# Dealing 1024 images to 128 partitions in two contiguous parts, with five loads, three stores and one more wait

## The chip, the cores and the metric

One core of a Trainium2 chip runs the kernel. The metric is device time in microseconds, the median of several executions. The kernel before takes 71.6 us. A change counts as faster or slower from 2% on.

A few words used throughout: a *transfer* is one load or store between HBM, the chip's main memory, and on-chip memory (SBUF); it is carried by 16 *transfer engines*, in *packets* (the 7 transfers of the kernel before make 1008 packets: for each, 128 of one partition's row and 16 of 4 bytes). Put in line by where one ends and the next begins, the 1008 records form 16 chains of 63, one for each engine: for each transfer 8 packets of a row and then one of 4 bytes (0.009 us), the transfers in the order of issue. The text calls this line of packets a *ring*; as the 16 are alike, it speaks of one. A transfer *lands* with the last of its 16 signals in the profile: those of the first load, whose last packets end at 8.88 to 9.25 us, come at 9.27 to 9.61 us. VectorE (DVE in the profile) is the engine that computes, SP the queue that issues the transfers. The *pitch* of a load is the distance in HBM between the rows of neighbouring partitions.

## The reference

```python
batch, channels, h, w = 16, 64, 32, 32
x        # (16, 64, 32, 32) float32
indices  # (16, 64, 32, 32), values 0 to 3; they reach the kernel as 64-bit integers
for b, c, i, j:                       # four nested loops
    idx = indices[b, c, i, j]
    output[b, c, 2 * i + idx // 2, 2 * j + idx % 2] = x[b, c, i, j]
# output: (16, 64, 64, 64) float32, zero elsewhere
```

There are 1024 images. One has 4 KiB of x, 8 KiB of indices and 16 KiB of result: 12 MiB to load in all and 16 MiB to store.

## The kernel before

Each partition has 8 images that lie together in HBM. For each of the four places in a 2x2 square, one VectorE instruction compares the indices with the place and multiplies by x. The parts that matter:

```python
G = 2; NG = T // G; FIRST = 3; N = H * W          # T = 8 images per partition
x_v = x.rearrange("b (ch t) h w -> (b ch) (t h w)", t=T)
idx_v = indices.rearrange("b (ch t) h w -> (b ch) (t h w)", t=T).bitcast(I32)
out_v = out.rearrange("b (ch g t) oh ow -> g (b ch) (t oh ow)", g=NG, t=G)
# ... (buffers and semaphores)
cut = FIRST * 2 * N
# issued ahead of the kernel's opening synchronisation, in this order:
nc.sync.dma_start(out=idx_t[:, :cut], in_=idx_v[:, :cut])     # 3 MiB, rows of 24 KiB, pitch 64 KiB
nc.sync.dma_start(out=x_t, in_=x_v)                           # 4 MiB, rows of 32 KiB
nc.sync.dma_start(out=idx_t[:, cut:], in_=idx_v[:, cut:])     # 5 MiB, rows of 40 KiB
# ... (semaphore increments and waits)
for t in range(T):                                 # one image, or two together
    for pidx in range(4):
        nc.vector.scalar_tensor_tensor(
            out=o_c[:, k : k + n, :, pidx // 2, :, pidx % 2],
            in0=idx_c[:, t : t + n], scalar=pidx, in1=x_c[:, t : t + n],
            op0=mybir.AluOpType.is_equal, op1=mybir.AluOpType.mult)
# ...
for g in range(NG):                                # four stores of two images per partition
    nc.sync.wait_ge(made, g + 1)
    nc.sync.dma_start(out=out_v[g], in_=out_t[g])
```

Of the kernel before, what the change touches and what calls it, by code (L numbers as in the profile page):

```python
# [1 line left out]

# [4 lines left out]

P = 128
F32 = mybir.dt.float32
I32 = mybir.dt.int32  # L10


class Program:




    def __init__(self, nc):
        self.nc = nc
        self.block = nc.main_func.blocks[0]  # L20
        self.kernel_block = nc.cur_bb.bb.name

    def __enter__(self):
        ins = self.block.instructions
        self.branches = [i for i in ins if "Branch" in type(i).__name__]
        n = len(ins) - len(self.branches)
        assert all("Branch" in type(ins[k]).__name__ for k in range(n, len(ins)))
        del ins[n:]
        self.nc.switch_bb(self.block.name, parent=None)
        self.symbolic = self.nc._always_lower_symbolic_ap  # L30
        self.nc._always_lower_symbolic_ap = False
        return self

    def first(self, made):
        ins = self.block.instructions
        assert ins[len(ins) - 1].name == made.ins.name
        moved = ins.pop()
        at = next(
            k
            for k, i in enumerate(ins)  # L40
            if i.engine == moved.engine and isinstance(i, mybir.InstDrain)
        )
        ins.insert(at, moved)

    def last(self, made):


        def move(nc):
            ins = self.block.instructions
            at = next(k for k, i in enumerate(ins) if i.name == made.ins.name)  # L50
            nc.main_func.blocks[-1].instructions.append(ins.pop(at))

        self.nc.at_finalize(move)

    def __exit__(self, kind, *_):
        self.nc._always_lower_symbolic_ap = self.symbolic
        if kind is None:
            for b in self.branches:
                self.block.instructions.append(b)
            self.nc.switch_bb(self.kernel_block, parent=None)  # L60


@with_exitstack
def kernel(
    ctx: ExitStack,
    tc: tile.TileContext,
    x: bass.AP,
    indices: bass.AP,
    kernel_size: bass.AP,
    out: bass.AP,  # L70
):
    nc = tc.nc
    assert kernel_size == 2

    B, C, H, W = x.shape
    n_img = B * C
    T = n_img // P
    assert T * P == n_img and C % T == 0

    G = 2  # L80
    NG = T // G
    FIRST = 3
    N = H * W
    x_v = x.rearrange("b (ch t) h w -> (b ch) (t h w)", t=T)
    idx_v = indices.rearrange("b (ch t) h w -> (b ch) (t h w)", t=T).bitcast(I32)
    out_v = out.rearrange("b (ch g t) oh ow -> g (b ch) (t oh ow)", g=NG, t=G)

    x_t = nc.alloc_sbuf_tensor("x_t", [P, T * N], F32).ap()
    idx_t = nc.alloc_sbuf_tensor("idx_t", [P, T * 2 * N], I32).ap()
    out_t = [  # L90
        nc.alloc_sbuf_tensor(f"out_t{g}", [P, G * 4 * N], F32).ap()
        for g in range(NG - 1)
    ]
    out_t.append(out_t[0])

    x_in = nc.alloc_semaphore("x_in")
    idx_in = [nc.alloc_semaphore(f"idx_in{g}") for g in range(2)]
    made = nc.alloc_semaphore("made")
    stored_0 = nc.alloc_semaphore("stored_0")
    stored = nc.alloc_semaphore("stored")  # L100

    x_c = x_t.rearrange("p (t i j) -> p t i j", t=T, j=W)
    idx_c = idx_t.rearrange("p (t i j two) -> p t i j two", t=T, j=W, two=2)[
        :, :, :, :, 0
    ]
    cut = FIRST * 2 * N

    with Program(nc) as program:
        program.first(
            nc.sync.dma_start(out=idx_t[:, :cut], in_=idx_v[:, :cut]).then_inc(  # L110
                idx_in[0], 16
            )
        )
        program.first(nc.sync.dma_start(out=x_t, in_=x_v).then_inc(x_in, 16))
        program.first(
            nc.sync.dma_start(out=idx_t[:, cut:], in_=idx_v[:, cut:]).then_inc(
                idx_in[1], 16
            )
        )

        nc.vector.wait_ge(x_in, 16).then_inc(x_in, -16)
        for t in range(T):
            g, k = t // G, t % G
            if t in (0, FIRST):
                half = int(t == FIRST)
                nc.vector.wait_ge(idx_in[half], 16).then_inc(idx_in[half], -16)  # L126


            if k == 1 and t != FIRST and g:
                continue  # L130
            n = 1 if k == 1 or t + 1 == FIRST or not g else 2
            if g == NG - 1:
                nc.vector.wait_ge(stored_0, 16).then_inc(stored_0, -16)
            o_c = out_t[g].rearrange(
                "p (m i two j wo) -> p m i two j wo", m=G, two=2, wo=2, j=W
            )
            for pidx in range(4):
                op = nc.vector.scalar_tensor_tensor(  # L138
                    out=o_c[:, k : k + n, :, pidx // 2, :, pidx % 2],
                    in0=idx_c[:, t : t + n],  # L140
                    scalar=pidx,
                    in1=x_c[:, t : t + n],
                    op0=mybir.AluOpType.is_equal,
                    op1=mybir.AluOpType.mult,
                )
            if k + n == G:
                op.then_inc(made, 1)

        for g in range(NG):
            nc.sync.wait_ge(made, g + 1)  # L150
            nc.sync.dma_start(out=out_v[g], in_=out_t[g]).then_inc(
                stored if g else stored_0, 16
            )
        nc.sync.sem_inc(made, -NG)
        program.last(
            nc.sync.wait_ge(stored, 16 * (NG - 1)).then_inc(stored, -16 * (NG - 1))
        )


# [1 line left out]
_INS = ['x', 'indices', 'kernel_size']  # L161
_OUTS = [((16, 64, 64, 64), 'float32')]

_NUMBERS = {'kernel_size': 2}


# [26 lines left out]
```

## Time and profile before

| | kernel before |
|---|---|
| device time, median | 71.6 us |
| span of the profiled execution | 70.2 us |
| share of the transfer engines' time that is filled | 97.6% |
| VectorE busy | 35.9 us |
| loads, stores | 3, 4 |

The prediction below shows the lines of the profile and reads them. In short: the ring of transfers is filled from 1 us to the end, from 5 us on at some 430 GB/s, and everything else is hidden behind it.

### The profile page before, as it was taken

What the parts mean: (1) busy time and instruction counts of PE and PEld (TensorE: products, weight loads), DVE (VectorE), ACT (ScalarE), POOL (GpSimd) and SP (SyncE); (2) the same over time, 40 slices, a digit from 0 to 9 for tenths busy, and PEclk for the clock granted to TensorE, in tenths of its full rate; (3) what the DMA queues carried; (4) which work ended last, traced back from release to release, by engine and by line L of the source; (5) the groups of instructions that cost most, each with busy time, mean ns of one, the idle gap of its engine ahead of it and who ended that gap; (6) DMA issues with size and microseconds to landing.
All of it is one profiled execution on the core that took longest, in us unless ns stands there. A gap on an engine that the chain in (4) does not pass through costs nothing.

```text
span 70.2 us, 76 instructions
## 1 busy us (share of the span) xinstructions
DVE 35.9 (51%) x24; POOL 0.2 (0%) x4
## 2 busy tenths in 40 slices
DVE  0000000000089999999999999999999500000000
POOL 1000000000000000000000000000000000000000
DMA  7699996979988899869999796969799896969692
GB/s 210 294 406 434 448 598 299 560 336 467 504 373 373 373 584 537 373 299 504 392 411 486 317 579 299 598 299 579 317 467 429 373 523 299 598 299 598 299 486 112
DMA packets 1008, 29.36 MB, mean 418 GB/s; under 512 B 112, under 2 KB 112, under 8 KB 112
## 3 DMA queue, kind: packets, MB, share of 16 engines
q1 hardware_dynamic: 1008, 29.36, 97.6%
HBM read 12.58 MB, written 16.78 MB: 418 GB/s over the span
## 4 chain that ended last, share of the span: by engine, by line
DVE 46%; DVEq 4%; issue 1%
DVE out_t L138 46%; DVEq L188 4%
## 5 line engine op out<-in xcount | busy, mean ns | idle before, releaser
L138 DVE SCALAR_TENSOR_TENSOR out_t<-idx_t,x_t 128x1024 f32<-128x1024 int32 (+1 forms) x24 | 35.9, 1574 | 19.6 <-DVEq L126 19.6
L174 POOL MEMSET const-bfloat16-1.0<- 128x1 bf16 x1 | 0.1, 101 | 0.0
L174 POOL MEMSET const-uint8-127<- 128x1 uint8 x1 | 0.1, 101 | 0.0
L174 POOL MEMSET const-float32-0.0<- 128x1 f32 x1 | 0.1, 98 | 0.2 <-issue 0.2
L174 POOL MEMSET const-float32-1.0<- 128x1 f32 x1 | 0.1, 98 | 0.0
## 6 DMA issues: line engine op xcount, KB each, us to landing
out_dram<-out_t SPq DMA_DIRECT2D x4, 4096.0 KB, 13.4
idx_t<-in_indices_dram SPq DMA_DIRECT2D x1, 5120.0 KB, 30.5
x_t<-in_x_dram SPq DMA_DIRECT2D x1, 4096.0 KB, 18.9
idx_t<-in_indices_dram SPq DMA_DIRECT2D x1, 3072.0 KB, 9.6
```

Source lines behind the costliest of these rows:

```text
L138: op = nc.vector.scalar_tensor_tensor(out=o_c[:, k : k + n, :, pidx // 2, :, pidx % 2], in0=idx_c[:, t : t + n], scalar=pidx, in1=x_c[:, t ...
L174: nc = _bacc.Bacc("TRN2", target_bir_lowering=False, num_devices=1)
L188: with _tile.TileContext(nc) as tc:
```

## The change

The intent, as the code has it, is to start VectorE earlier (after 4.5 MiB instead of 7), to make each part one contiguous piece of HBM with fewer and longer store packets, and to hold the first store back until the second-last load has landed.

```diff
-    x_v = x.rearrange("b (ch t) h w -> (b ch) (t h w)", t=T)
-    idx_v = indices.rearrange("b (ch t) h w -> (b ch) (t h w)", t=T).bitcast(I32)
-    out_v = out.rearrange("b (ch g t) oh ow -> g (b ch) (t oh ow)", g=NG, t=G)
+    A, Z = 3, 5
+    Z1, Z2 = 2, 3
+    def sections(ap):
+        flat = ap.rearrange("b ch h w -> (b ch) (h w)")
+        return [
+            part.rearrange("(p t) n -> p (t n)", t=t)
+            for part, t in ((flat[: A * P], A), (flat[A * P :], Z))
+        ]
     ... (one input buffer, in which the last results take the place of inputs)
+        for tile_, hbm, sem in (
+            (idx_a, idx_v[0], in_a),
+            (x_a, x_v[0], in_a),
+            (x_z, x_v[1], in_z),
+            (idx_z[:, :last_idx], idx_v[1][:, :last_idx], in_z),
+            (idx_z[:, last_idx:], idx_v[1][:, last_idx:], in_last),
+        ):
+            program.first(nc.sync.dma_start(out=tile_, in_=hbm).then_inc(sem, 16))
     ... (VectorE: 4 instructions on 3 images, 4 on 2, 4 on 2, 4 on 1)
+        for k, dst in enumerate(stores):
+            nc.sync.wait_ge(made, k + 1)
+            if k == 0:
+
+                nc.sync.wait_ge(in_z, 32)
+            nc.sync.dma_start(out=dst, in_=out_t[k]).then_inc(stored, 16)
```

The loads now have pitches of 24, 12, 20 and 40 KiB; the first one, still 24 KiB per row, has its pitch changed from 64 KiB to 24.

More of the change, by code (lines that the diff above doesn't have):

```diff
@@ L76 @@
     n_img = B * C
-    T = n_img // P
-    assert T * P == n_img and C % T == 0
-    G = 2
-    NG = T // G
-    FIRST = 3
-    N = H * W
-    x_v = x.rearrange("b (ch t) h w -> (b ch) (t h w)", t=T)
-    idx_v = indices.rearrange("b (ch t) h w -> (b ch) (t h w)", t=T).bitcast(I32)
-    out_v = out.rearrange("b (ch g t) oh ow -> g (b ch) (t oh ow)", g=NG, t=G)
-    x_t = nc.alloc_sbuf_tensor("x_t", [P, T * N], F32).ap()
-    idx_t = nc.alloc_sbuf_tensor("idx_t", [P, T * 2 * N], I32).ap()
+    N = H * W
@@ new lines @@
+    A, Z = 3, 5
+    Z1, Z2 = 2, 3
+    assert (A + Z) * P == n_img and Z1 + Z2 == Z
+    def sections(ap):
[4 more added lines that the diff above has]
+        ]
+    x_v = sections(x)
+    idx_v = [v.bitcast(I32) for v in sections(indices)]
+    out_v = sections(out)
+    inputs = nc.alloc_sbuf_tensor("inputs", [P, (A + Z) * 3 * N], F32).ap()
@@ L90 @@
+    idx_a = inputs[:, : A * 2 * N].bitcast(I32)
+    x_a = inputs[:, A * 2 * N : A * 3 * N]
+    idx_z = inputs[:, A * 3 * N : (A * 3 + Z * 2) * N].bitcast(I32)
+    x_z = inputs[:, (A * 3 + Z * 2) * N :]
+    assert Z2 * 4 <= A * 3 + Z1 * 2
     out_t = [
-        nc.alloc_sbuf_tensor(f"out_t{g}", [P, G * 4 * N], F32).ap()
-        for g in range(NG - 1)
-    ]
-    out_t.append(out_t[0])
-    x_in = nc.alloc_semaphore("x_in")
-    idx_in = [nc.alloc_semaphore(f"idx_in{g}") for g in range(2)]
+        nc.alloc_sbuf_tensor("out_a", [P, A * 4 * N], F32).ap(),
+        nc.alloc_sbuf_tensor("out_z", [P, Z1 * 4 * N], F32).ap(),
+        inputs[:, : Z2 * 4 * N],
+    ]
@@ L98 @@
+    stores = [
+        out_v[0],
+        out_v[1][:, : Z1 * 4 * N],
+        out_v[1][:, Z1 * 4 * N :],
+    ]
+    last_idx = (Z - 1) * 2 * N
+    in_a = nc.alloc_semaphore("in_a")
+    in_z = nc.alloc_semaphore("in_z")
+    in_last = nc.alloc_semaphore("in_last")
     made = nc.alloc_semaphore("made")
-    stored_0 = nc.alloc_semaphore("stored_0")
     stored = nc.alloc_semaphore("stored")
-    x_c = x_t.rearrange("p (t i j) -> p t i j", t=T, j=W)
-    idx_c = idx_t.rearrange("p (t i j two) -> p t i j two", t=T, j=W, two=2)[
-        :, :, :, :, 0
-    ]
@@ L106 @@
-    cut = FIRST * 2 * N
-    with Program(nc) as program:
-        program.first(
-            nc.sync.dma_start(out=idx_t[:, :cut], in_=idx_v[:, :cut]).then_inc(
-                idx_in[0], 16
-            )
-        )
-        program.first(nc.sync.dma_start(out=x_t, in_=x_v).then_inc(x_in, 16))
-        program.first(
-            nc.sync.dma_start(out=idx_t[:, cut:], in_=idx_v[:, cut:]).then_inc(
-                idx_in[1], 16
-            )
-        )
-        nc.vector.wait_ge(x_in, 16).then_inc(x_in, -16)
-        for t in range(T):
-            g, k = t // G, t % G
-            if t in (0, FIRST):
-                half = int(t == FIRST)
-                nc.vector.wait_ge(idx_in[half], 16).then_inc(idx_in[half], -16)
-            if k == 1 and t != FIRST and g:
-                continue
-            n = 1 if k == 1 or t + 1 == FIRST or not g else 2
-            if g == NG - 1:
-                nc.vector.wait_ge(stored_0, 16).then_inc(stored_0, -16)
-            o_c = out_t[g].rearrange(
-                "p (m i two j wo) -> p m i two j wo", m=G, two=2, wo=2, j=W
+    work = (
+        (x_a, idx_a, 0, A, 0, 0),
+        (x_z, idx_z, 0, Z1, 1, 0),
+        (x_z, idx_z, Z1, Z2 - 1, 2, 0),
+        (x_z, idx_z, Z - 1, 1, 2, Z2 - 1),
+    )
@@ new lines @@
+    with Program(nc) as program:
+        for tile_, hbm, sem in (
[6 more added lines that the diff above has]
+            program.first(nc.sync.dma_start(out=tile_, in_=hbm).then_inc(sem, 16))
+        for k, (x_s, idx_s, lo, n, o, at) in enumerate(work):
+            if k == 0:
+                nc.vector.wait_ge(in_a, 32).then_inc(in_a, -32)
+            elif k == 1:
+                nc.vector.wait_ge(in_z, 32)
+            elif k == 2:
+                nc.vector.wait_ge(made, 2)
+            else:
+                nc.vector.wait_ge(in_last, 16).then_inc(in_last, -16)
+            x_c = x_s[:, lo * N : (lo + n) * N].rearrange("p (i j) -> p i j", j=W)
+            idx_c = idx_s[:, lo * 2 * N : (lo + n) * 2 * N].rearrange(
+                "p (i j two) -> p i j two", j=W, two=2
+            )[:, :, :, 0]
+            o_c = out_t[o][:, at * 4 * N : (at + n) * 4 * N].rearrange(
+                "p (i two j wo) -> p i two j wo", two=2, wo=2, j=W
@@ L138 @@
                 op = nc.vector.scalar_tensor_tensor(
-                    out=o_c[:, k : k + n, :, pidx // 2, :, pidx % 2],
-                    in0=idx_c[:, t : t + n],
+                    out=o_c[:, :, pidx // 2, :, pidx % 2],
+                    in0=idx_c,
                     scalar=pidx,
-                    in1=x_c[:, t : t + n],
+                    in1=x_c,
                     op0=mybir.AluOpType.is_equal,
@@ L145 @@
                 )
-            if k + n == G:
+            if k != 2:
                 op.then_inc(made, 1)
-        for g in range(NG):
-            nc.sync.wait_ge(made, g + 1)
-            nc.sync.dma_start(out=out_v[g], in_=out_t[g]).then_inc(
-                stored if g else stored_0, 16
-            )
-        nc.sync.sem_inc(made, -NG)
-        program.last(
-            nc.sync.wait_ge(stored, 16 * (NG - 1)).then_inc(stored, -16 * (NG - 1))
-        )
+        for k, dst in enumerate(stores):
+            nc.sync.wait_ge(made, k + 1)
+            if k == 0:
+                nc.sync.wait_ge(in_z, 32)
+            nc.sync.dma_start(out=dst, in_=out_t[k]).then_inc(stored, 16)
+        nc.sync.sem_inc(made, -3)
+        nc.sync.sem_inc(in_z, -32)
+        program.last(nc.sync.wait_ge(stored, 48).then_inc(stored, -48))
 _INS = ['x', 'indices', 'kernel_size']
```

## The prediction

No term of the sum is among them: it came to -0.06 us (0.04 for one more transfer, -0.15 for the start, +0.05 for a gap), so 71.5 us. That the steady rate (433 GB/s from 10 to 20 us) stays what it was is the assumption. The 0.005 us fixed per packet are an estimate from the trace before: a 32 KiB packet takes 1.213 us, four times the 0.301 us from 32 to 40 KiB are 1.204, and the records of neighbouring packets overlap by 0.004.

> **What bounds the kernel now.** I read the page from the top: busy shares, slices, the queue line, then the chain, then the waits and the list of transfers.
>
> ```profile
> span 70.2 us, 76 instructions
> DVE 35.9 (51%) x24; POOL 0.2 (0%) x4
> ...
> DVE  0000000000089999999999999999999500000000
> ...
> DMA  7699996979988899869999796969799896969692
> ...
> q1 hardware_dynamic: 1008, 29.36, 97.6%
> HBM read 12.58 MB, written 16.78 MB: 418 GB/s over the span
> ```
>
> VectorE, the only engine that computes, works 35.9 of 70.2 us, all in the middle. The one transfer queue fills 97.6% of the time of its 16 engines. The strip of slices says the same of each moment: no slice after the second is below 6 tenths but the last (a packet is counted in the slice where it starts, so the digits swing). The stretches, with the transfer engines' share and GB/s in the last two columns, are steadier:
>
> ```profile
> 0.00:5.00 5.00, 0.00 (x0) 0.20 (x4) 1.00 0.84 315
> 5.00:10.00 5.00, 0.00 (x0) 0.00 (x0) 1.00 0.97 419
> 10.00:20.00 10.00, 0.44 (x1) 0.00 (x0) 1.00 1.00 433
> ```
>
> Only the first 5 us are poor, 315 GB/s. From 5 us on loads and stores follow each other at some 430 GB/s. The list of transfers gives the time from issue to landing:
>
> ```profile
> out_dram<-out_t SPq DMA_DIRECT2D x4, 4096.0 KB, 13.4
> idx_t<-in_indices_dram SPq DMA_DIRECT2D x1, 5120.0 KB, 30.5
> x_t<-in_x_dram SPq DMA_DIRECT2D x1, 4096.0 KB, 18.9
> idx_t<-in_indices_dram SPq DMA_DIRECT2D x1, 3072.0 KB, 9.6
> ```
>
> and the timeline of the queue that issues gives the issues:
>
> ```profile
> 0.00 0.38 SPq L110 DMA_DIRECT2D idx_t<-in_indices_dram  x1
> 0.43 0.43 SPq L114 DMA_DIRECT2D x_t<-in_x_dram  x1
> 0.91 0.43 SPq L116 DMA_DIRECT2D idx_t<-in_indices_dram  x1
> 28.76 27.03 SPq L151 DMA_DIRECT2D out_dram<-out_t  x4
> ```
>
> Added up, the loads land at 9.6, 19.3 and 31.4 us. The first store is issued at 28.76, 2.6 us before the last load lands, and lands 12.4 us later at 41.2; the last is issued at 55.5 and lands 14.7 us later at 70.2, the end. So between 9.6 and 70.2 us one transfer lands after another with none missing: 9.7 us for each 4 MiB, load or store alike, 12.1 us for 5 MiB. One more MiB costs 2.41 us, and a transfer costs some 0.04 us besides (9.68 less 4 x 2.41; taken from the packet records, where a 32 KiB packet takes 1.213 us, a 40 KiB one 1.514 us and a semaphore packet 0.009 us). The chain of waits that the page prints ends in VectorE at 55.4 us and gives it 46%; I do not follow it. It stops at what released the last store, but that store was ready long before its turn: it was issued at 55.5, when the store ahead of it still had until about 60.4 to run. VectorE has nearly 5 us of slack at the end, and the path is the transfers alone.
>
> The time is then: 1.03 us from the first issue to the first packet, 28 MiB at 2.41 us each (67.5), 7 transfers at 0.04 (0.3), a slow start, and 0.45 us from the last packet to the end of the span. The slow start is what is left: 70.2 - 1.03 - 67.5 - 0.3 - 0.45 = 0.9 us. The packet records show most of it: the first 16 packets of 24 KiB, one on each engine, took 1.4 to 1.8 us, some of the next 1.0 to 1.4, all others 0.912; that is 0.55 us per engine. The rest, near 0.4 us, is that the engines do not begin all at once. The timed runs are 1.4 us above the span (71.6 to 70.2), which I take as unchanged.
>
> [...]433 GB/s in the stretch from 10 to 20 us, and 2.41 us per MiB is 435.[...] the store issued at 28.76 moved its first packet at 30.66, when the earliest engine was done with the last load. So a store's earlier issue gains nothing while loads lie ahead.[...]
>
> **The change part by part.**
>
> Bytes: none removed, none added. Loads 12 MiB, stores 16 MiB; 28 x 2.41 us stays.
>
> Transfers: 3 loads and 4 stores become 5 loads and 3 stores, 8 for 7: +0.04 us. Packets become 24, 12, 20, 32 and 8 KiB for the loads, 48, 32 and 48 KiB for the stores; at 0.005 us fixed per packet that is inside the 0.04.
>
> Start: the first transfer is again 3 MiB in 24 KiB packets. It now reads one contiguous piece, rows 24 KiB apart instead of 64. If the slow first packets come from the pitch, up to 0.5 us goes; if they come from starting cold, nothing. The trace can't tell, since it has one start. I give 40% to some gain and book -0.15 us.
>
> New load schedule, for the slowest engine, from the same 9.25 us for the end of the first packets: 1.5 MiB of x 3.66 us, to 12.9; 2.5 MiB of x 6.07 us, to 19.0; 4 MiB of indices 9.68 us, to 28.65; 1 MiB 2.45 us, to 31.1. For the earliest engine each is 0.37 us sooner, so it is free at 30.7.
>
> Wait of VectorE: it starts after 4.5 MiB instead of 7. A landing is seen about 0.5 us after its last packet (the load of x: last packet 18.93, VectorE's first instruction 19.56). So it begins near 13.5 instead of 19.6. This gain is off the path.
>
> VectorE's work: 24 instructions become 16. From the groups by shape, 18.3 us for 16 of 1024 elements is 1.14 us each, 17.7 for 8 of 2048 is 2.21; so 1.07 per 1024 elements plus 0.07. Four of 3072 take 3.28 each, 13.1 us: done at 26.6. Four of 2048 begin when the fourth load has landed, 29.2, and end at 38.0; four more end at 46.9, and the last image's four of 1024 at 51.5. All off the path if the stores find their data ready.
>
> Stores: the first needs its data (26.6) and, newly, the second-last load (seen at 29.2). The added wait is the later by 2.6 us. Issue at 29.25; from an issue to a first packet the trace's start has 1.03 us, so 30.3. The earliest engine is done with loads at 30.7: 0.4 us to spare, so the wait costs nothing, narrowly. It was 0.9 us before (28.76 + 1.03 against 30.66). The second store is ready at 38.1, and the first runs until 31.1 + 6 MiB (14.5) = 45.6: 7 us to spare. The third is ready at 51.6 and the second runs to 45.6 + 9.7 = 55.3: over 2 us to spare after the 1.03. The third then takes 14.5, to 69.8; with 0.45 that is a span of 70.25, 0.05 above the present one.
>
> Sum: 0.04 for the extra transfer, -0.15 expected from the start, +0.05 for the chance that the 0.4 us at the turn from loads to stores is not enough: -0.06, so **71.5 us**.
>
> **The rivals.**
>
> A gap at the turn. The new wait puts the issue of the first store about 2 us ahead of the end of loads, and only 0.4 us of it is slack. For it: a store's first packet may need longer than the first load's, and the issuing queue has two waits to pass. Against: the spread between the engines helps, and the same 1.03 us held at the start with nothing prepared. I give a gap 20%; it would cost 0.1 to 0.5 us, so 71.7 to 72.1.
>
> A better start.[...] Against: the other loads and all stores, at pitches of 32 to 128 KiB, show no slow packet. It would give 71.0 to 71.2.
>
> VectorE sets the end. Its chain now has two waits in the middle, for the fourth load and for its own second part (the third part's results go where inputs lay). It would need to be 2.6 us later than worked out to delay the third store. Its working is from measured durations, so under 5%; 72 to 73.
>
> Long issues. Five loads are issued before the kernel's opening synchronisation, at 0.43 us each; 2.3 us against VectorE's start at 13.5. If the queue took no more than a few transfers at a time, the fifth issue would hang until the first has landed, near 9.6 us; still early enough.
>
> **The range and the chances.** Start gain (to -0.5) and gap (to +0.5) are the two unknowns, each the smaller part of the odds; with 0.1 us of scatter between runs that makes 71.0 to 72.0 for 8 in 10. Faster by over 2% means under 70.2 us. Take away the whole slow start of 0.55 us and 71.05 is left[...]: 2%. Slower by over 2% means over 73.0, a gap of 1.5 us or slow packets in the new layout: 3%. Within 2%: 95%.
>
> **What would show it.** Right: a queue share of 97 to 98%; loads landing near 13.4, 29.1 and 31.6; first store issued near 29.2, stores landing near 46, 55.7 and 70.2; VectorE starting at 13.5 with an idle stretch of some 2.6 us before its fifth instruction. Better start: the first 5 us above 315 GB/s and every landing earlier by the same amount. A gap: a slice near 31 us with a low transfer digit, and the stores' landings later than the last load's by more than 14.6, 24.2 and 38.7 us. Wrong altogether: 48 KiB packets that take more than some 1.8 us (1.514 + 0.301), which would make writing slower than the ring's rate, or VectorE as the one who releases the last store late.

## The result, and the profile after

| | before | after |
|---|---|---|
| median of 6 runs | 71.57 us (71.44 to 71.69) | 72.13 us (71.87 to 72.26) |
| span of the profiled execution | 70.2 us | 70.9 us |

The ratio is 1.0078, with a 95% interval of 1.0057 to 1.0098. It is the mean time of one kernel's fast runs over that of the other's of the same rounds, so not quite the ratio of the two medians. The change is within 2%, as most of the chances said, but it loses some 0.56 us where 0.1 us of gain was predicted, and 72.13 lies above the predicted range, which ended at 72.0.

First the page of the changed kernel: the busy shares, the strip of VectorE and that of the transfers, and the queue's line.

```profile
span 70.9 us, 69 instructions
DVE 35.5 (50%) x16; POOL 0.2 (0%) x4
...
DVE  0000000099999993299999999999940000000000
...
DMA  9599999999999798899999999789898999999990
...
q1 hardware_dynamic: 1152, 29.36, 97.1%
```

VectorE starts three slices earlier and rests for two in the middle, as planned. The queue is as full as before, and no slice near 31 us (the 17th to 19th) is low: no gap opened between loads and stores. Next the stretches of the changed kernel (the last two columns are the transfer engines' share and GB/s):

```profile
0.00:5.00 5.00, 0.00 (x0) 0.20 (x4) 1.00 0.84 295
5.00:10.00 5.00, 0.00 (x0) 0.00 (x0) 1.00 0.95 408
10.00:20.00 10.00, 5.95 (x2) 0.00 (x0) 1.00 1.02 438
```

Only the first two are worse than before: 295 GB/s against 315, then 408 against 419. The engines are as busy in the first 5 us (0.84 in both kernels), but move less: their packets take longer. The transfers of the changed kernel, with the time from issue to landing last, and the issues of the timeline:

```profile
out_dram<-out_a SPq DMA_DIRECT2D x1, 6144.0 KB, 16.9
out_dram<-inputs SPq DMA_DIRECT2D x1, 6144.0 KB, 18.7
inputs<-in_indices_dram SPq DMA_DIRECT2D x1, 4096.0 KB, 28.3
out_dram<-out_z SPq DMA_DIRECT2D x1, 4096.0 KB, 17.7
inputs<-in_indices_dram SPq DMA_DIRECT2D x1, 3072.0 KB, 10.2
inputs<-in_x_dram SPq DMA_DIRECT2D x1, 2560.0 KB, 19.1
inputs<-in_x_dram SPq DMA_DIRECT2D x1, 1536.0 KB, 13.5
inputs<-in_indices_dram SPq DMA_DIRECT2D x1, 1024.0 KB, 30.1
```

```profile
0.00 0.38 SPq L136 DMA_DIRECT2D inputs<-in_indices_dram  x1
0.43 0.90 SPq L136 DMA_DIRECT2D inputs<-in_x_dram  x2
1.38 1.22 SPq L136 DMA_DIRECT2D inputs<-in_indices_dram  x2
29.80 0.35 SPq L171 DMA_DIRECT2D out_dram<-out_a  x1
38.66 0.34 SPq L171 DMA_DIRECT2D out_dram<-out_z  x1
52.14 0.33 SPq L171 DMA_DIRECT2D out_dram<-inputs  x1
```

All five loads are issued by 2.60 us, so no issue waited for a landing. The first load is the line of 3072 KB. It is issued at 0 us in both kernels and lands at 10.2 us instead of 9.6. That is about the whole loss, and it is there before VectorE, the stores or the added wait have acted. From then on all goes to the predicted intervals: the stores land at 46.7, 56.4 and 70.8 us (issue plus landing time), 9.7 us and 14.5 us apart, as was worked out. For the turn from loads to stores the packet records are plain: the earliest transfer engine ended its last load at 30.91 us and its part of the first store at 45.41, the slowest at 31.75 and 46.25. Both took 14.50 us, just what 6 MiB take. No gap, and no slow packet, lay between.

The packet records also show what the 0.6 us are. To compare kernels I use one number, the *start lag*: when the slowest engine has done its part of the first load, less the time that its packets take at the steady rate (7.27 us for rows of 24 KiB). It is 1.98 us before and 2.62 us after. Of it, 1.0 us is the wait for the first packet; the rest is a first packet that takes 1.0 to 1.8 us before and 1.0 to 2.4 us after, instead of 0.912, and that engines do not start at once (their first packets begin at 1.03 to 1.82 us before, at 1.03 to 1.74 after). In the mean of the 16 engines the first packet grew only from 1.45 to 1.68 us; it is the slowest engine that sets the end. The engines never make up for this: the slowest one keeps its distance to the end, 69.75 us before and 70.44 after. One transfer more costs 0.04 us by the prediction's estimate (two cost 0.09 in the run with five loads below). The difference of the profiled executions, 72.21 less 71.51 us, is nearly these two: 0.64 and 0.04.

### The profile page after: what moved, and what is told of

It reads as the page before. It is cut to its first block, busy times and chain, and to the rows that moved or that the text cites. A ratio compares the mean times of both kernels' runs of the same rounds, so it can differ in the third digit from the quotient of the medians.

```text
span 70.9 us, 69 instructions
## 1 busy us (share of the span) xinstructions
DVE 35.5 (50%) x16; POOL 0.2 (0%) x4
## 4 chain that ended last, share of the span: by engine, by line
DMA 40%; DVE 25%; DVEq 6%; SPq 2%; issue 1%
DMA inputs<-in_indices_dram 40%; DVE inputs L155 13%; DVE out_z L155 13%; DVEq L205 6%; SPq L136 2%
## 5 line engine op out<-in xcount | busy, mean ns | idle before, releaser
L155 DVE SCALAR_TENSOR_TENSOR out_a<-inputs 128x3072 f32<-128x3072 int32 x4 | 13.2, 3354 | 14.0 <-DVEq L140 14.0
L155 DVE SCALAR_TENSOR_TENSOR inputs<-inputs 128x2048 f32<-128x2048 int32 (+1 forms) x8 | 13.4, 1753 | 0.0
L155 DVE SCALAR_TENSOR_TENSOR out_z<-inputs 128x2048 f32<-128x2048 int32 x4 | 8.9, 2286 | 2.5 <-DMA inputs<-in_indices_dram 2.5
## 6 DMA issues: line engine op xcount, KB each, us to landing
inputs<-in_indices_dram SPq DMA_DIRECT2D x1, 3072.0 KB, 10.2
inputs<-in_x_dram SPq DMA_DIRECT2D x1, 1536.0 KB, 13.5
inputs<-in_indices_dram SPq DMA_DIRECT2D x1, 1024.0 KB, 30.1
```

Source lines behind the costliest of these rows:

```text
L155: op = nc.vector.scalar_tensor_tensor(out=o_c[:, :, pidx // 2, :, pidx % 2], in0=idx_c, scalar=pidx, in1=x_c, op0=mybir.AluOpType.is_equal ...
```

## The experiments

Eighteen kernels ran, in groups that share one chip and the runs of the kernel before, each timed in 5 rounds; the kernel before had medians of 71.43 to 71.58 us in these groups. By the 2% rule one of them is slower (the changed kernel without its wait), one unclear (the merged last loads without the wait), and all others are the same; the smaller differences below rest on the 95% intervals. The diffs are shortened. Where an experiment reads other addresses than it should, its result is wrong; that other values alone change nothing is seen in the run with an offset (ratio 0.9996, the same packets).

### Is it the first load's addresses, or the number of loads issued at the start?

Theory A: the pitch of the first load makes the first packets slow. Theory B: five issues instead of three disturb them. Four runs cross the two.

**The kernel before with a contiguous first load** (wrong):

```diff
-            nc.sync.dma_start(out=idx_t[:, :cut], in_=idx_v[:, :cut])
+            nc.sync.dma_start(out=idx_t[:, :cut], in_=idx_first)
+    # idx_first: images 0 to 383, "(p t) n -> p (t n)", t=3: pitch 24 KiB
```

> The kernel before, but the first load reads the first 3 MiB of the indices as one contiguous piece (rows 24 KiB apart) instead of 24 KiB of every 64 KiB; same destination, same packets; the result is wrong on purpose. Theory A (the address pattern of the first load sets how slow the first packets are): the last engine finishes its first nine packets near 9.9 us instead of 9.25, and the time is about 72.1 us, 0.5 over the kernel before. Theory B (five loads issued at the start instead of three disturb the first packets): no change, 71.6.

Measured: 71.99 us, ratio to before 1.0071 (1.0052 to 1.0089); start lag 2.40 us. One address pattern in one load makes most of the loss. Its first load took 10.0 us to land, for 9.6:

```profile
idx_t<-in_indices_dram SPq DMA_DIRECT2D x1, 3072.0 KB, 10.0
```

**The changed kernel with the old first load** (wrong):

```diff
-            (idx_a, idx_v[0], in_a),
+            (idx_a, idx_first, in_a),
+    # idx_first: 24 KiB of every 64 KiB, as in the kernel before
```

> The changed kernel, but its first load reads 24 KiB of every 64 KiB as the kernel before does; the result is wrong on purpose. Theory A: last engine near 9.25 us, time about 71.6 us. Theory B: no change from the changed kernel, about 72.1.

Measured: 71.68 us, ratio to before 1.0013 (1.0000 to 1.0026); start lag 1.95 us. The loss is gone. The first two stretches of this run, and its first load:

```profile
0.00:5.00 5.00, 0.00 (x0) 0.20 (x4) 1.00 0.84 315
5.00:10.00 5.00, 0.00 (x0) 0.00 (x0) 1.00 0.97 418
```

```profile
inputs<-in_indices_dram SPq DMA_DIRECT2D x1, 3072.0 KB, 9.6
```

315 GB/s and 9.6 us are the kernel before's own figures, in the changed kernel with all its other loads, stores and waits.

**The changed kernel with two loads issued later** (right result):

```diff
+        nc.sync.wait_ge(in_i, 16)          # the first load has landed
+        nc.sync.dma_start(out=idx_z[:, :last_idx], ...)
+        nc.sync.dma_start(out=idx_z[:, last_idx:], ...)
     ... (taken out of the five loads that are issued at the start)
```

> The changed kernel with a right result, but its fourth and fifth load are issued only when the first has landed (near 10 us, with two loads still queued), so that just three are issued at the start. Theory A: no change, about 72.1. Theory B: the first packets are as in the kernel before, last engine near 9.25 us, time about 71.6.

Measured: 72.12 us, ratio 1.0079 (1.0059 to 1.0098), start lag 2.63 us: as the changed kernel. Three issues at the start were as slow as five.

**The kernel before with five loads** (right result):

```diff
-        program.first(nc.sync.dma_start(out=x_t, in_=x_v).then_inc(x_in, 16))
-        program.first(nc.sync.dma_start(out=idx_t[:, cut:], in_=idx_v[:, cut:])...)
+        # x in two loads (1.5 and 2.5 MiB), the second part of the indices in two (4 and 1 MiB)
```

> The kernel before with its own layout, but the loads cut in five (3 MiB of indices, x in 1.5 and 2.5 MiB, indices in 4 and 1 MiB), all issued at the start as in the changed kernel. Theory A: no change but 0.08 us for two more transfers, about 71.65. Theory B: about 72.1.

Measured: 71.64 us, ratio 1.0013 (1.0002 to 1.0025), start lag 1.98 us. Two more transfers cost 0.09 us by the ratio (0.01 to 0.18 by its interval); 0.08 was expected. Theory B falls in both directions, and theory A holds in both.

### Which pitches are bad?

I first held that engines that start farther apart in memory do better (A1), against a rule that only distances that are powers of two do (A2). The runs are the kernel before with the first load's 24 KiB rows taken at other pitches, all wrong, of this form:

```diff
+    idx_first = indices as "(p t) n -> p (t n)" with t = 6 (or 4, 5, 7), first 24 KiB of each row
-            nc.sync.dma_start(out=idx_t[:, :cut], in_=idx_v[:, :cut])
+            nc.sync.dma_start(out=idx_t[:, :cut], in_=idx_first)
```

> The kernel before, its first load reading 24 KiB of every 48 KiB; wrong on purpose. Theory A1 (what counts is how far apart in memory the 16 engines start; the further, the better): between the kernel before and the contiguous read but near the former, about 71.7 us. Theory A2 (a distance that is a power of two, 64 KiB, is what does well): as the contiguous read, about 72.0.

> The kernel before, its first load reading 24 KiB of every 32 KiB; wrong on purpose. Theory A1: not far from the contiguous read, 71.85 to 72.0. Theory A2: as the kernel before, 71.6.

> The kernel before, its first load reading 24 KiB of every 40 KiB; wrong on purpose. If only powers of two between rows (32, 64 KiB) do well: slow, 71.9 to 72.4. If 24 and 48 KiB are bad for being multiples of three: 71.6.

> The kernel before, its first load reading 24 KiB of every 64 KiB, but the second 24 KiB instead of the first, so that no packet starts at a multiple of 16 KiB; wrong on purpose. If the distance between rows counts: 71.55. If the alignment of the packets' starts counts: as the contiguous read, 71.9 or more.

> The kernel before, its first load reading 24 KiB of every 56 KiB; wrong on purpose. The rule so far (32 and 64 KiB good, 24, 40 and 48 bad) says slow: 71.9 to 72.5 us. If a wide spread helps after all, 71.6.

| pitch of the first load | median us | ratio to before | start lag us |
|---|---|---|---|
| 24 KiB (contiguous) | 71.99 | 1.0071 | 2.40 |
| 32 KiB | 71.66 | 1.0018 | 2.15 |
| 40 KiB | 72.36 | 1.0127 | 2.89 |
| 48 KiB | 72.41 | 1.0127 | 2.88 |
| 56 KiB | 71.45 | 1.0007 | 1.89 |
| 64 KiB (the kernel before) | 71.43 to 71.58 | 1 | 1.98 |
| 64 KiB, from the 24th KiB on | 71.46 | 0.9996 | 2.01 |

Each start lag is that of one profiled execution. Over all kernels with these 24 KiB rows it was 1.95 to 2.14 us at 64 KiB (eight kernels) and 2.30 to 2.63 at 24 KiB (five), so 2.15 alone would not tell 32 KiB from 64; its ratio does. Within that the start lag orders the times, so the loss is where the theory puts it: nearly all of it at each engine's first packet. By the packet records of these runs, the loads' packets from an engine's third on took what they take in the kernel before (0.912 us for 24 KiB, 1.213 for 32, 1.514 for 40), but for single ones (at most 0.16 us longer) and the turn to the stores. But both rules fall: 48 KiB is worse than 24 though it is wider, and 56 KiB is as good as 64 though it is no power of two. Whether the rows start at multiples of 16 KiB made no difference either (last line, ratio 0.9996). The first loads of three runs in the list of transfers, for 48, 56 and 64 KiB with the offset in this order, show it without the packet records:

```profile
idx_t<-in_indices_dram SPq DMA_DIRECT2D x1, 3072.0 KB, 10.5
```

```profile
idx_t<-in_indices_dram SPq DMA_DIRECT2D x1, 3072.0 KB, 9.6
```

```profile
idx_t<-in_indices_dram SPq DMA_DIRECT2D x1, 3072.0 KB, 9.6
```

That the pitch is the cause is shown, for rows from the start of the index tensor (in the last line 24 KiB further on); the rule by which some pitches are bad stays open. In the traces of 40 and 48 KiB a single engine was far behind (its first packet ended at 3.81 and 3.80 us, the next latest at 3.16 and 3.45); why is not shown.

**x first** (right result), the first two loads of the kernel before in the other order:

```diff
-        program.first(idx_t[:, :cut] load)
         program.first(x_t load)
+        program.first(idx_t[:, :cut] load)
```

> The kernel before with the whole x as the first load (4 MiB, one contiguous piece, packets of 32 KiB) and the first part of the indices second; the result is right. Theory A1: slow first packets, about 71.9 us. Theory A2: about 71.6. If only the index tensor's memory were concerned: 71.6 too.

Measured: 71.70 us, ratio 1.0028 (1.0015 to 1.0040), start lag 2.22 us. A contiguous piece with a pitch of 32 KiB loses 0.2 us, close to the 0.13 us of the gapped 32 KiB in the table. It lay between the two expectations and decided nothing alone.

**A smaller first load** (right result), the first load of the kernel before cut into 1 MiB and 2 MiB:

```diff
+        for lo, hi in ((0, 2 * N), (2 * N, cut)):      # rows of 8 KiB, then 16 KiB
```

> The kernel before with its first load cut in two: 1 MiB in packets of 8 KiB, then 2 MiB; result right. If the first packet of each engine is slow in proportion to its bytes (0.55 us of 24 KiB), the slow start shrinks to a third and the time is 71.6 + 0.04 - 0.35 = 71.3 us; if the start is slow for a stretch of time (until about 2.5 us) whatever the packets, 71.6 to 71.65.

Measured: 71.61 us, ratio 1.0016 (1.0002 to 1.0029), start lag 1.91 us. The first packets took 0.80 us in the mean instead of 0.31 for 8 KiB, an excess of 0.49 us, against 0.53 us for 24 KiB rows in the kernel before. The excess was nearly the same for both sizes: here it is a delay at the start, not a low rate, and a small first piece did not cut it down.

### Is there anything else in the change that costs?

**The changed kernel with the old dealing**, all else kept (right result):

```diff
-        flat = ap.rearrange("b ch h w -> (b ch) (h w)")
-        return [part.rearrange("(p t) n -> p (t n)", t=t) for part, t in (...)]
+        whole = ap.rearrange("b (ch t) h w -> (b ch) (t h w)", t=A + Z)
+        cut = whole.shape[1] // (A + Z) * A
+        return [whole[:, :cut], whole[:, cut:]]
```

> The changed kernel with everything kept (five loads, three stores, the added wait, VectorE's parts) but the dealing: each partition has 8 images that lie together, of which the first 3 and the last 5 make the two parts, so loads have rows 32 or 64 KiB apart and stores 128 KiB apart, as in the kernel before; result right. If the dealing alone made the loss: first load as in the kernel before (slowest engine about 1.95 us behind a steady stream), time 71.55 to 71.65. If something else of the change has a part in it: nearer 72.1.

Measured: 71.70 us, ratio 1.0018 (1.0002 to 1.0034), start lag 2.12 us in the profiled run. Of the 0.56 us the dealing makes 0.43 (1.0078 less 1.0018, times 71.5); the other 0.13 (0.01 to 0.24 by the interval) hold 0.04 for the transfer.

**Two contiguous parts of 512 images**, four stores of 4 MiB (right result):

```diff
-    A, Z = 3, 5
-    Z1, Z2 = 2, 3
+    A, Z = 4, 4
+    Z1, Z2 = 2, 2
     ... (part A computed and stored in two halves, one more output buffer)
```

> The changed kernel dealt out in two contiguous parts of 512 and 512 images, with five loads and four stores of 4 MiB; every row is then a multiple of 16 KiB and the first load's rows are 32 KiB apart; result right. If what is bad is a distance between rows that is no power of two, and not that the parts are contiguous: 71.6 to 71.8 us. If contiguity itself is bad: 72.1.

Measured: 71.87 us, ratio 1.0065 (1.0050 to 1.0081), start lag 2.29 us. Neither expectation was met: the pitch of 32 KiB loses less here than 24 KiB did, but not nothing, and two transfers more than before cost 0.08 us of the 0.46. I don't read more from it.

### The added wait

The prediction held that the wait is hidden. The direct test:

```diff
             nc.sync.wait_ge(made, k + 1)
-            if k == 0:
-                nc.sync.wait_ge(in_z, 32)
             nc.sync.dma_start(out=dst, in_=out_t[k]).then_inc(stored, 16)
```

> The changed kernel without the first store's added wait for the second-last load; result right. The store is then issued near 27.4 us instead of 29.8. If the wait is hidden, as the landings say: no change from the changed kernel, 72.1 within 0.1. If it costs: up to 0.3 us faster.

Measured: 73.31 us (72.73 to 73.80), ratio to before 1.0242 (1.0203 to 1.0281): 1.2 us *slower* than with the wait. Both expectations missed. The issue of the first store, and the last load with its time from issue to landing, in this run (29.80 us and 30.1 with the wait):

```profile
27.10 0.35 SPq L168 DMA_DIRECT2D out_dram<-out_a  x1
```

```profile
inputs<-in_indices_dram SPq DMA_DIRECT2D x1, 1024.0 KB, 30.8
```

The store comes 2.7 us earlier and the last load, which it is queued behind, takes 0.7 us longer. By the packet records, the last load's 8 KiB packets took 0.31 us with the wait and, from 29.1 us on, up to 0.79 us without it, together 0.67 us per engine. The profiled execution (72.73 us) was the quickest of the six; where the slower five lost more was not recorded, so the "all of it" in the next expectation goes beyond the record.

Two more kernels ask what makes the load vulnerable. **The old dealing without the wait** (right result; the two edits above together):

> The changed kernel with the old dealing and without the added wait; result right. Removing the wait in the new dealing cost 1.2 us over the changed kernel, all of it in the 8 KiB packets of the last load, which took 0.35 to 0.79 us instead of 0.31. Theory S (small packets of a load suffer when a store is queued right behind them, wherever they lie in memory): slow again, 72.4 to 73.2 us. Theory D (it is again the place in memory: rows 40 KiB apart): no loss, 71.6 to 71.75.

Measured: 72.72 us, ratio 1.0183 (1.0170 to 1.0197), against 1.0018 with the wait. The place in memory is not the cause (theory D falls).

**No wait, and the last two loads made one** (right result):

```diff
-            (idx_z[:, :last_idx], idx_v[1][:, :last_idx], in_z),
-            (idx_z[:, last_idx:], idx_v[1][:, last_idx:], in_last),
+            (idx_z, idx_v[1], in_z),
     ... (the added wait taken out as above, and VectorE's wait for the last load)
```

> The changed kernel without the added wait and with the last two loads made one (packets of 40 KiB instead of 32 and 8), the store issued near 27 us as early as without the wait; result right. Theory S: no slow packets at the turn, 72.1 us as the changed kernel. If a store queued early slows loads of any packet size: 72.6 to 73.3.

Measured: 72.88 us, ratio 1.0213 (1.0192 to 1.0234), 1.0 us above the changed kernel by the ratios. Now the 40 KiB packets are slow, the last of each engine, up to 2.66 us instead of 1.514. Small packets are not the cause either (theory S falls). What is left is the early store itself. To test that away from the new stores and buffers, **the kernel before with an early VectorE** (right result): its own dealing and four stores, five loads, and one semaphore for each part of x, so that the first two images are ready early:

```diff
-    x_in = nc.alloc_semaphore("x_in")
+    x_in = [nc.alloc_semaphore(f"x_in{g}") for g in range(2)]
     ... (loads as in the run with five loads)
-        nc.vector.wait_ge(x_in, 16)                  # all of x, before image 0
+        nc.vector.wait_ge(x_in[half], 16)            # the first part before image 0, the second before image 3
```

> The kernel before (its dealing, its four stores of 4 MiB) with the five loads of the run before_five_loads and a semaphore for each part of x, so that VectorE starts near 13.4 us instead of 19.6 and the first store is issued near 22.5 us instead of 28.8, with some 8.5 us of loads still ahead in the ring; result right. Theory E (a store that is in the ring long before the loads ahead of it are done slows the last of those loads): the last loads' packets take longer than their 0.31 us, 72.5 to 73.3 us. If the loss belonged to the new stores (48 KiB packets) or to the new buffers: 71.6.

Measured: 72.80 us, ratio 1.0177 (1.0161 to 1.0194). And **the same with the wait**:

```diff
             nc.sync.wait_ge(made, g + 1)
+            if g == 0:
+                nc.sync.wait_ge(idx_in[1], 16)
             nc.sync.dma_start(out=out_v[g], in_=out_t[g])
```

> The same, but the first store also waits until the second-last load has landed (issue near 29.2 us); VectorE starts as early as in i1; result right. Theory E: no slow packets, 71.55 to 71.7 us. If VectorE's early work beside the loads is what slows them: as i1.

Measured: 71.60 us, ratio 1.0008 (0.9995 to 1.0021). The stores' issues (the first number is that of the first of four) and the last load with its time from issue to landing, without the wait and then with it:

```profile
22.90 29.00 SPq L162 DMA_DIRECT2D out_dram<-out_t  x4
```

```profile
idx_t<-in_indices_dram SPq DMA_DIRECT2D x1, 1024.0 KB, 30.7
```

```profile
29.20 22.55 SPq L164 DMA_DIRECT2D out_dram<-out_t  x4
```

```profile
idx_t<-in_indices_dram SPq DMA_DIRECT2D x1, 1024.0 KB, 29.6
```

Holding the store back by 6.3 us brings the load in 1.1 us sooner and the kernel's end 1.2 us sooner. VectorE works just as early in both (from 13.7 and 13.6 us), so it is the store in the ring that counts. Loads did not do this to loads: in the kernel before all are issued by 1.34 us, the first lands at 9.6, and from an engine's third on every load packet takes 0.912, 1.213 or 1.514 us by its size. Nor did stores to stores: the second store of the kernel before was issued at 37.84 us, 3.3 us before the first had landed, and no packet of 32 KiB took more than 1.284 us instead of 1.213. In the kernel before the first store is issued at 28.76 us, 2.6 us before the last load lands, and it escapes: not one load packet is slow at its turn (all the last load's take 1.514 us). The least early store that did full harm is that of the changed kernel without the wait, issued at 27.10 us where the last load lands near 32 us when it is undisturbed. Between 2.6 and some 5 us ahead of the loads' end, then, the harm set in with these kernels. The lower end may be near: with the small first load the store was issued 2.7 us before the last load landed, and in its one profiled execution six of the 16 engines' last 40 KiB packets took 1.52 to 1.78 us instead of 1.514, while with x first and with five loads, at 2.7 and 2.8 us, none was slow. A still earlier store did not do more harm: issued 8.7 us ahead of the undisturbed landing (22.90 us, the kernel before with an early VectorE) it cost 1.2 us as well, and there the packets of the second-last load, up to 28.6 us, kept their 1.213 us; only the last 3 to 4 us of the loads were slow, as in the changed kernel without the wait. What happens inside the engines in that time is not shown.

No version with a right result beat the kernel before: the nearest is the last one, equal to it within its interval.

## Why the prediction was right or wrong

- *What bounds the kernel* was right. In every profile the ring stayed 96.7 to 97.9% filled, and where something was found to move the time it was packets slower than the others, besides some 0.04 us for each added transfer.
- *The start* is the step that failed. The prediction booked -0.15 us for it, "I give 40% to some gain", and none of its rivals had the sign turned: the "better start" rival took the contiguous read for the better one or for a neutral one, and slow packets in the new layout were named only as part of the 3% for a loss of over 2%. It measured +0.64 us in the start lag of the profiled run, and some +0.4 us in the timed runs with the dealing alone. What the runs showed in its place: the contiguous first load makes the first packets slower, not faster (the kernel before with that load alone lost 0.5 us, the changed kernel with the old first load lost next to nothing). Two things were wrong. The trace before had one start and one pitch, so it could not show the sign, and a loss at the start had no place in the sum. And the stake was taken as the mean excess of 0.55 us per engine, while the slowest engine sets the end: the mean first packet grew by 0.23 us, the start lag by 0.64. The prediction also read 1.4 to 1.8 us for the 16 first packets; they took 1.0 to 1.8, and those of 1.0 to 1.4 that it put among the next are first packets of engines that began late. With +0.64 in the place of -0.15 the same sum, without its +0.05 for a gap, gives 71.6 + 0.04 + 0.64 = 72.28, near the 72.13 measured and the 72.21 of the profiled run.
- *Transfers*: 0.04 us each agrees with the run with five loads, where two more cost 0.09 us (0.01 to 0.18).
- *The turn from loads to stores* was right. The gap rival did not occur: 14.50 us on the earliest and on the slowest engine. The store's issue (29.80 for 29.25) and the last load are both later by about the 0.6 us of the start, so the slack stayed.
- *VectorE* was right: 13.2 us for the first part (13.1 worked out), and an idle stretch of 2.5 us (2.6). It starts at 14.05 us instead of 13.5, the slow start again. It released no store late.
- *The added wait*: "the wait costs nothing" was right, but the reasoning that went with it, that "a store's earlier issue gains nothing while loads lie ahead", missed half. It does not only gain nothing: it lost 1.2 us in each of three pairs of kernels that differ in the wait alone (73.31 and 72.13; by the ratios 1.0183 and 1.0018; 1.0177 and 1.0008), the last pair on the kernel before's own stores. The wait is what keeps the earlier VectorE from doing harm.

## What to carry to other kernels

The ring of transfers was filled from start to end here (96.7 to 97.9%), and work that was ready earlier was worth nothing: with VectorE's start at 13.6 us instead of 19.6 the kernel before took 71.60 us for 71.58. It hurt (1.2 us) where it put a store behind loads too soon, so in a kernel like this try to hold the first store back, as the added wait did here, until some 2.4 us before the last load lands. A delay of one engine's first packet was never made up (the slowest engine ended 0.69 us later for 0.64 us at the start), so try the address pattern of the very first load as a parameter of its own; it moved the time by 0.9 us here with the same bytes and packets. An ablation that changes only the addresses, with a wrong result, settled that question here with two runs, one on each kernel.
